# The first feed-forward product of a hybrid decoder block, 24 of its 32 column tiles by Strassen's seven products

## The chip, the cores and the metric

The kernel runs on one core of a Trainium2 chip. The metric is the time of one execution in microseconds of the device. A core has a matrix engine (TensorE), VectorE, ScalarE, GpSimd and SyncE (SP), whose queue issues all data transfers here. The engines run at the same time, each in the order in which its instructions were issued, and wait for one another by semaphores. TensorE adds its products up in eight banks (PSUM) of 128 partitions by 512 numbers; everything else lies in the on-chip memory (SBUF).

## What is computed

One decoder layer on 512 tokens of width 1024: token mixing (a gated unit and sparse attention), cross-attention into 256 memory tokens, and a feed-forward part. The change concerns the last:

```python
D_MODEL, SEQ, D_FF = 1024, 512, 4096
h = rms_norm(x, norm_ffn_g[l])                                    # (512, 1024)
x = x + jnp.square(jax.nn.relu(h @ w_ff1[l])) @ w_ff2[l]          # w_ff1 1024 x 4096, w_ff2 4096 x 1024
```

All inputs and the output are float32.

## The kernel before

**Numbers.** TensorE's operands are tiles of the type fp32r. Each operand is split into a high part, the number cast to that type, and a low part, the rest (a subtraction on VectorE). A product of two split operands is three matmuls: high by high, high by low, low by high (`mm3`). `split_any` lets the cast go to ScalarE or VectorE; the low part is always VectorE's.

**Order.** The program is written down as a list of operations. The class `Plan` gives each a cost (`cost`), a start from the engines' and buffers' state, and places those with a choice (`nc.either`) on the engine that is done first. `LEADS` moves the priority of single stages; its keys are the names of stages. `issue` then sends out the instructions in the order that came out, so that nearly all carry the same line number in the profile (L412), and groups are told apart by the tiles' names.

**Buffers.** `raw` (3) holds a weight block of 128x1024 as loaded, `w` (4, `WRING`) its two parts. `b8` (11 of 8 KB a partition) holds large tiles: the transposed hidden input, the residual, the hidden activations. `q` (4), `z` (6), `P` (6) and `bT` (2) hold tiles 512 wide. `SHARE` says how many of each kind a part of the program (its queue) may hold for sure.

**Feed-forward.** `ch_f(t)` norms token tile t (128 tokens), transposes it and splits it into `h3h` and `h3l`, each two tiles of four 128-row blocks by 512 tokens. For each of the 32 column tiles f of `w_ff1` (128 columns), `granule` loads 1024x128 weights and splits them, `ff1` multiplies, 8 k-blocks by 3 terms with 512 tokens as moving columns: 24 matmuls into one bank. ScalarE takes the relu out of the bank into a `z` tile, and the square goes to ScalarE or VectorE and into `hid[f]`. The first two column tiles (`ff_a`, `ff_b`) are computed in two halves of 256 tokens, as fillers of the cross-attention's waits. The first-product matmuls carry the names `ps<-b,w` (512 columns) and, for the fillers, `ps<-b,b` (256 columns; attention has that name too).

The second product keeps eight banks `accs` (four token tiles by two halves of the width). For each f it loads `w_ff2`'s rows (`load_ff2`), splits them and `hid[f]` (a `qpair`), and adds 8 x 3 matmuls (`part`, `ps<-w,q`). The last two f are taken bank by bank, and each finished bank is scaled, added to the residual in `xs[t]` and stored:

```python
dve.scalar_tensor_tensor(xv[:, c:c + n], accs[2 * t + blk][:, c:c + n], rf[t], xv[:, c:c + n], OP.mult, OP.add)
dma(out[0, t * P:t * P + P, blk * 512 + c:blk * 512 + c + n], xv[:, c:c + n])
```

Of the kernel before, what the change touches and what calls it, by code (L numbers as in the profile page):

```python
# [9 lines left out]
F32 = mybir.dt.float32  # L10
# [7 lines left out]
P = 128  # L18
# [19 lines left out]
WRING = 4  # L38
QLEAD = 200
# [17 lines left out]
LEADS = {"ch_f0": -304, "ch_norm3": -5448, "ch_o0": 500, "ch_o0.w512.2": 3108, "ch_o1": -1711,  # L57
# [17 lines left out]


class Plan:
# [60 lines left out]
    def cost(self, eng, op, aps, func):  # L138
        n = max(self.width(a) for a, _ in aps)
        if eng == "tensor":  # L140
            if op == "transpose" and all(a.dtype == F32 for a, _ in aps):
                return 109
            return max(25, n / 2.4 + (15 if n > 200 else 7))
# [272 lines left out]
def hybrid_block(ctx, tc, x, mem, norm_mix_g, w_in, sg_ln_g, sg_ln_b, sg_w, sg_b, q_norm_g,  # L416
# [10 lines left out]
    spool = ctx.enter_context(tc.tile_pool(name="small", bufs=1))  # L427
    pps = ctx.enter_context(tc.tile_pool(name="ps", bufs=8, space=PS))
# [15 lines left out]
    def qpair():  # L444
        t = zpool.tile([P, 2, 512], F32R, tag="q", bufs=4, name=nm("q"))
        return t[:, 0, :], t[:, 1, :]

    def b8(shape, dt):
        n = 1
        for s in shape[1:]:  # L450
            n *= s
        assert n <= SB8
        t = bpool.tile([P, n], dt, tag="b8", bufs=11, name=nm("b8"))
        if len(shape) == 3:
            return t.rearrange("p (a b) -> p a b", a=shape[1])
        if len(shape) == 4:
            return t.rearrange("p (a b c) -> p a b c", a=shape[1], b=shape[2])
        return t
# [213 lines left out]
    KL = cpool.tile([P, NKV, 2, T], F32R, name="KL")  # L672
# [145 lines left out]
    Vc = cpool.tile([P, NKV, G, P], F32R, name="Vc")  # L818
# [404 lines left out]
    rf = [None] * TT  # L1223
    def ch_norm(t):
        h2 = b8([P, 2, KT, P], F32R)
        st[t]['h2'] = h2
        norm_T(xs[t], g_mem, [h2[:, 0, 0:4, :], h2[:, 0, 4:8, :]], [h2[:, 1, 0:4, :], h2[:, 1, 4:8, :]])
        e = small(1)
        dve.tensor_scalar(e, stats(xs[t], D), EPS / D, EPS * EPS, OP.mult, OP.add)
        st[t]['e'] = e  # L1230
# [106 lines left out]

    hid = []

    def hid_tile(f):  # L1340
        if f < FT - 4:
            if f % 4 == 0:
                t = b8([P, 4, T], F32)
                hid.extend(t[:, i, :] for i in range(4))
        else:
            hid.append(zpool.tile([P, 512], F32, tag="P", bufs=6, name=nm("hid")))
        return hid[f]
# [29 lines left out]
    for f in range(NFILL, FT):  # L1377
        nc.stage = f"ff{f}"
        hid_tile(f)
        ff1(f, granule(w1v[:, :, f * P:f * P + P]), 0, T)  # L1380

# [4 lines left out]
    def load_ff2(f):  # L1386
        (w,) = granule(w2v[:, f:f + 1, :])
        hh, hl = qpair()
        split_any(hid[f], hh, hl)
        ff2[f] = hh, hl, w  # L1390

    def part(f, t, blk):
# [3 lines left out]
            start=f == 0, stop=f == FT - 1)  # L1396

    for f in range(FT - LAST):
        load_ff2(f)
        for t in range(TT):  # L1400
            for blk in range(2):
                part(f, t, blk)
    for f in range(FT - LAST, FT):
        load_ff2(f)
    for t in range(TT):
        for blk in range(2):
            for f in range(FT - LAST, FT):
                part(f, t, blk)
            xv = xs[t][:, blk * 512:blk * 512 + 512]
# [37 lines left out]
```

## Time and profile before

| | |
|---|---|
| median of 3 runs | 697.59 us (696.68 to 697.99) |
| the profiled execution | 696.73 us, its span from the first to the last instruction 695.0 us |
| TensorE busy, matmuls | 688.1 us (99%), 3600 |
| VectorE, ScalarE, GpSimd busy | 420.8 us (61%), 307.7 us (44%), 80.5 us (12%) |
| loaded and stored | 68.32 MB and 2.10 MB, 101 GB/s over the span |

In the profile PE is a matmul, PEld the load of its weights (the stationary operand), DVE is VectorE, ACT ScalarE, POOL GpSimd, SPq the queue of transfers. A name such as `ps<-b,w` is output, moving operand, stationary operand for a matmul. Matmuls are pipelined: the duration of one is longer than the step to the next, so steps are read from starts.

### The profile page before, as it was taken

The page shows a single profiled execution, that of the slowest core. Times are in us where ns is not written, and L with a number is a line of the kernel's source. Part 1 is how long each engine was busy: PE and PEld are TensorE (multiplying, and loading weights), DVE is VectorE, ACT ScalarE, POOL GpSimd, SP SyncE. Part 2 cuts the span into 40 slices and gives each one's busy share as a digit, 9 for nine tenths or more (in the row PEclk, how much of TensorE's full clock was granted, in tenths as well). Part 3 has the DMA queues.
Part 4 walks back from the last instruction along what each step waited for, and adds up shares of the span by engine and source line. Part 5 has one row for each costly group of instructions (what it writes and reads, how often), then busy time and mean ns, then how long its engine had stood idle before and what let it go on. Part 6 is the DMA issues. An engine that isn't in the chain of part 4 may idle for free.

```text
span 695.0 us, 9606 instructions
## 1 busy us (share of the span) xinstructions
PE 688.1 (99%) x3600; PEld 583.3 (84%) x3600; DVE 420.8 (61%) x832; ACT 307.7 (44%) x622; POOL 80.5 (12%) x121
## 2 busy tenths in 40 slices
PE   8999999999999999999999999999999999999997
PEld 7898887888899888889888888888888888888886
DVE  5698799988999997588832533332233444334433
ACT  6453575977789774677431522221151221112210
POOL 1102123133332230213100000000000000000000
PEclk9999999999999999999999999999999999999999
DMA  8632574560221101323243333333233222333203
GB/s 269 181 112 77 158 203 135 202 188 2 91 92 61 62 1 34 119 62 91 68 112 97 88 95 106 103 91 91 92 108 104 91 91 91 101 109 94 91 1 121
DMA packets 63678, 71.03 MB, mean 102 GB/s; under 512 B 3160, under 2 KB 46928, under 8 KB 63632
## 3 DMA queue, kind: packets, MB, share of 16 engines
q1 hardware_dynamic: 63632, 70.42, 32.8%
q8 instruction: 28, 0.46, 0.3%
q14 instruction: 18, 0.15, 0.1%
HBM read 68.32 MB, written 2.10 MB: 101 GB/s over the span
## 4 chain that ended last, share of the span: by engine, by line
PE 98%; DVE 1%; DMA 1%; ACT 0%; issue 0%; SPq 0%; DVEq 0%
PE ps L412 98%; DMA raw<-in_w_in_dram 1%; DVE b L412 0%; DVE w L412 0%; ACT w L412 0%; SPq L412 0%; ACT z L412 0%; DVEq L1442 0%
## 5 line engine op out<-in xcount | busy, mean ns | idle before, releaser
L412 PE MATMUL ps<-w,q 128*128 128x512 f32 x960 | 224.7, 391 | 0.0
L412 PEld LDWEIGHTS ps<-w,q 128*128 128x128 f32 x960 | 178.9, 188 | 36.4 <-ACT q L412 0.2
L412 PE MATMUL ps<-w,b 128*128 128x512 f32 (+2 forms) x832 | 184.6, 375 | 0.1
L412 DVE TENSOR_TENSOR w<-raw,w 128x1024 fp32r<-128x1024 f32 (+2 forms) x113 | 132.8, 1178 | 69.4 <-ACT w L412 68.4
L412 ACT CAST w<-raw 128x1024 fp32r<-128x1024 f32 (+2 forms) x80 | 82.2, 1029 | 206.7 <-PE ps L412 201.9
L412 PE MATMUL ps<-b,w 128*128 128x512 f32 x720 | 167.1, 390 | 0.0
L412 PEld LDWEIGHTS ps<-w,b 128*128 128x128 f32 (+1 forms) x832 | 143.7, 186 | 25.7 <-DVE w L412 0.6
L412 PEld LDWEIGHTS ps<-b,w 128*128 128x128 f32 x720 | 134.7, 188 | 28.4 <-ACT z L412 0.5
L412 DVE TENSOR_TENSOR b<-ps,b 128x512 fp32r<-128x512 f32 (+2 forms) x88 | 54.7, 636 | 11.2 <-ACT b L412 8.2
L412 PE MATMUL ps<-b,b 128*128 128x256 f32 (+1 forms) x344 | 59.1, 291 | 0.0
L412 DVE CAST q<-b 128x512 fp32r<-128x512 f32 (+1 forms) x28 | 11.7, 418 | 75.8 <-PE ps L412 75.8
L412 ACT CAST b<-ps 128x512 fp32r<-128x512 f32 (+1 forms) x84 | 43.9, 548 | 20.5 <-PE ps L412 20.3
L412 DVE CAST w<-raw 128x1024 fp32r<-128x1024 f32 (+2 forms) x33 | 21.5, 652 | 51.4 <-PE ps L412 51.1
L412 ACT ACTIVATE z<-ps 128x512 f32<-128x512 f32 (+3 forms) x43 | 23.6, 580 | 62.8 <-PE ps L412 62.8
L412 PEld LDWEIGHTS ps<-b,b 128*128 128x128 f32 x344 | 48.0, 190 | 1.5 <-DVE b L412 0.2
L412 POOL TENSOR_SCALAR P<-P,s,gates 128x128 f32<-128x128 f32 (+3 forms) x56 | 35.6, 645 | 96.0 <-DVE s L412 62.0
L412 POOL TENSOR_TENSOR r<-s,negh 128x1 f32<-128x1 f32 (+2 forms) x25 | 23.4, 939 | 106.2 <-DVE s L412 106.2
L412 PE MATMUL ps<-idf,P 128*128 128x128 f32 x192 | 30.9, 276 | 0.0
L412 PE MATMUL ps<-b,q 128*128 128x256 f32 (+2 forms) x96 | 25.8, 334 | 0.3 <-ACT q L412 0.3
L412 PEld LDWEIGHTS ps<-idf,P 128*128 128x128 f32 x192 | 22.5, 141 | 2.4 <-POOL P L412 0.3
L412 DVE TENSOR_TENSOR q<-b,q 128x512 fp32r<-128x512 f32 (+1 forms) x36 | 23.5, 656 | 1.4 <-ACT q L412 0.5
L412 ACT ACTIVATE P<-P,s 128x384 f32<-128x384 f32 (+1 forms) x32 | 21.6, 676 | 1.8 <-DVE s L412 1.5
(156 smaller groups left out, 561.2 us busy)
## 6 DMA issues: line engine op xcount, KB each, us to landing
raw<-in_w_ff_dram SPq DMA_DIRECT2D x64, 512.0 KB, 3.7
raw<-in_w_in_dram SPq DMA_DIRECT2D x12, 512.0 KB, 4.5
raw<-in_cmp_w_dram SPq DMA_DIRECT2D x8, 512.0 KB, 4.3
raw<-in_w_out_dram SPq DMA_DIRECT2D x8, 512.0 KB, 4.1
raw<-in_w_mkv_dram SPq DMA_DIRECT2D x8, 512.0 KB, 4.4
b<-in_x_dram SPq DMA_DIRECT2D x8, 256.0 KB, 5.2
raw<-in_w_in_dram SPq DMA_DIRECT2D x8, 256.0 KB, 5.5
b<-in_x_dram SPq DMA_DIRECT2D x4, 512.0 KB, 7.0
```

The source lines that it names most:

```text
L412: getattr(getattr(self.nc, eng), op)(*a, **k)
```

## The change

Column tiles 8 to 31 are taken four at a time. The hidden input is cut into two halves of the tokens (256) and two of k (512), the weights of four column tiles into two halves of k and two of the columns (256), and the 2x2 product of blocks is made of seven products in place of eight (Winograd's order, with sums S1 to S4 of the input, made once, and three running sums of the weights in each group). A product (`prod`) is 2 column tiles by 4 k-blocks by 3 terms, 24 matmuls of 256 columns into one bank. Four banks serve a group; three of the seven products are added onto a bank that has been read before. The sums of products are made by VectorE out of the banks, relu and square follow (`relu2`).

Each weight block (512x256, 512 KB) is loaded and, as it is or as a sum, split: seven splits in a group in place of four. The residual `xs[t]` is written to DRAM (`xq`) behind `ch_f(t)` and read back into new tiles (`xr`) for the end. The hidden tiles lie in `bT`, `P`, `b8`, `q` and a gain row's buffer; the second product takes f in the order 20 to 27, 0 to 19, 28 to 31, and its first eight splits of `hid` use `b8` tiles. `b8` has 12 buffers in place of 11 and `q` 5 in place of 4; `KL` and `Vc` of the attention, which had tiles of their own, use these. `LEADS` is new throughout, and the plan's cost of a matmul of 201 to 300 columns is 4 ns less.

```diff
--- before.py
+++ after.py
@@ -36,6 +36,8 @@
 LAST = 2
 NWARM = 28
 WRING = 4
+
+FONE = 8
 QLEAD = 200
 SB8 = 2048
 
@@ -54,24 +56,30 @@
          "wa": dict(w=3, raw=2),
          "wf": dict(w=1, raw=1)}
 
-LEADS = {"ch_f0": -304, "ch_norm3": -5448, "ch_o0": 500, "ch_o0.w512.2": 3108, "ch_o1": -1711,
...
+LEADS = {"ch_f0": -3007, "ch_norm0": -637, "ch_norm1": -2138, "ch_norm2": 916, "ch_norm3": 2082,
...
 
 
 class Plan:
@@ -140,7 +148,7 @@
         if eng == "tensor":
             if op == "transpose" and all(a.dtype == F32 for a, _ in aps):
                 return 109
-            return max(25, n / 2.4 + (15 if n > 200 else 7))
+            return max(25, n / 2.4 + (15 if n > 300 else 11 if n > 200 else 7))
         if eng == "sync":
             run = min(list(a.ap)[-1][1] for a, _ in aps)
             return max(450, 4 * n * max(list(a.ap)[0][1] for a, _ in aps) / (230 if run <= 128 else 290))
@@ -425,6 +433,7 @@
     bpool = ctx.enter_context(tc.tile_pool(name="big", bufs=1))
     zpool = ctx.enter_context(tc.tile_pool(name="z", bufs=1))
     spool = ctx.enter_context(tc.tile_pool(name="small", bufs=1))
+    dpool = ctx.enter_context(tc.tile_pool(name="dram", bufs=1, space=bass.MemoryType.DRAM))
     pps = ctx.enter_context(tc.tile_pool(name="ps", bufs=8, space=PS))
 
     dma = nc.sync.dma_start
@@ -442,7 +451,7 @@
         return zpool.tile([P, 512], dt, tag="z", bufs=6, name=nm("z"))
 
     def qpair():
-        t = zpool.tile([P, 2, 512], F32R, tag="q", bufs=4, name=nm("q"))
+        t = zpool.tile([P, 2, 512], F32R, tag="q", bufs=5, name=nm("q"))
         return t[:, 0, :], t[:, 1, :]
 
     def b8(shape, dt):
@@ -450,7 +459,7 @@
         for s in shape[1:]:
             n *= s
         assert n <= SB8
-        t = bpool.tile([P, n], dt, tag="b8", bufs=11, name=nm("b8"))
+        t = bpool.tile([P, n], dt, tag="b8", bufs=12, name=nm("b8"))
         if len(shape) == 3:
             return t.rearrange("p (a b) -> p a b", a=shape[1])
         if len(shape) == 4:
@@ -669,7 +678,7 @@
 
 
     KB = b8([P, NKV, 2, T], F32R)
-    KL = cpool.tile([P, NKV, 2, T], F32R, name="KL")
+    KL = b8([P, NKV, 2, T], F32R)
     for h in range(NKV):
         pool.memset(KL[(1 - h) * HD:(2 - h) * HD, h].bitcast(F32), 0.0)
     VB = b8([P, 2 * NKV * TT, P], F32R)
@@ -815,7 +824,9 @@
 
     nc.lead, nc.stage = 0, "cmp"
 
-    Vc = cpool.tile([P, NKV, G, P], F32R, name="Vc")
+    Vc = zpool.tile([P, 1024], F32R, tag="q", bufs=5, name="Vc")
+    nc.home[Vc.tensor.name] = "gain"
+    Vc = Vc.rearrange("p (h g d) -> p h g d", h=NKV, g=G)
     pool.memset(Vc.bitcast(F32), 0.0)
 
     cps = bank().rearrange("p (i c) -> p i c", i=2)
@@ -1221,6 +1232,7 @@
     g_ffn = h3h = h3l = wq = wmo = None
     st = [dict() for _ in range(TT)]
     rf = [None] * TT
+    xq = [dpool.tile([P, D], F32, name=f"xq{t}") for t in range(TT)]
     def ch_norm(t):
         h2 = b8([P, 2, KT, P], F32R)
         st[t]['h2'] = h2
@@ -1335,15 +1347,29 @@
         rf[t] = cpool.tile([P, 1], F32, name=f"rf{t}")
         dve.tensor_tensor(rf[t], r, r, OP.mult)
 
+        dma(xq[t], xs[t])
+
     hid = []
 
+    def hid_tiles(f):
+
+        if f < 2:
+            return [zpool.tile([P, 512], F32, tag="bT", bufs=2, name=nm("hid")) for _ in range(2)]
+        if f < 8:
+            return [zpool.tile([P, 512], F32, tag="P", bufs=6, name=nm("hid")) for _ in range(6)]
+        if f < 20:
+            t = b8([P, 4, T], F32)
+            return [t[:, i, :] for i in range(4)]
+        t = [zpool.tile([P, 2, 512], F32, tag="q", bufs=5, name=nm("hid")) for _ in range(1 if f == 28 else 2)]
+        if f == 28:
+            g = cpool.tile([P, 2, 512], F32, tag="gain", bufs=1, name=nm("hid"))
+            nc.home[g.tensor.name] = "gain"
+            t.append(g)
+        return [v[:, i, :] for v in t for i in range(2)]
+
     def hid_tile(f):
-        if f < FT - 4:
-            if f % 4 == 0:
-                t = b8([P, 4, T], F32)
-                hid.extend(t[:, i, :] for i in range(4))
-        else:
-            hid.append(zpool.tile([P, 512], F32, tag="P", bufs=6, name=nm("hid")))
+        while len(hid) <= f:
+            hid.extend(hid_tiles(len(hid)))
         return hid[f]
 
     def ff1(f, ws, c0, n):
@@ -1374,18 +1400,135 @@
     nc.queue, nc.stage = "ff", "ff"
 
 
-    for f in range(NFILL, FT):
+    for f in range(NFILL, FONE):
         nc.stage = f"ff{f}"
         hid_tile(f)
         ff1(f, granule(w1v[:, :, f * P:f * P + P]), 0, T)
 
+
+    def quarter(th, kh):
+        c = slice(th * 2 * P, th * 2 * P + 2 * P)
+        return h3h[kh][:, :, c], h3l[kh][:, :, c]
+
+    def half(t, i):
+        return t[:, i, :].rearrange("p (k n) -> p k n", k=4)
+
+    def either_tt(out, a, b, op):
+        nc.either(("vector", "tensor_tensor"), ("gpsimd", "tensor_tensor"))(out, a, b, op)
+
+    nc.stage = "ffs"
+    X, Y, Z = (b8([P, 2, 1024], F32) for _ in range(3))
+    A22, A21, A11, A12 = quarter(1, 1), quarter(1, 0), quarter(0, 0), quarter(0, 1)
+    for t, i, (h, l) in ((X, 0, A21), (X, 1, A22), (Y, 0, A11), (Y, 1, A12)):
+        either_tt(half(t, i), h.bitcast(F32), l.bitcast(F32), OP.add)
+    sums = []
+
+    def keep(t, i):
+        w = b8([P, 2, 1024], F32R)
+        split_any(t[:, i, :], w[:, 0, :], w[:, 1, :])
+        sums.append((half(w, 0), half(w, 1)))
+
+    either_tt(Z[:, 0, :], X[:, 0, :], X[:, 1, :], OP.add)
+    keep(Z, 0)
+    either_tt(Z[:, 1, :], Z[:, 0, :], Y[:, 0, :], OP.subtract)
+    keep(Z, 1)
+    either_tt(X[:, 0, :], Y[:, 0, :], X[:, 0, :], OP.subtract)
+    keep(X, 0)
+    either_tt(Y[:, 1, :], Y[:, 1, :], Z[:, 1, :], OP.subtract)
+    keep(Y, 1)
+    S1, S2, S3, S4 = sums
+
+    def raw4():
+        t = wpool.tile([P, 1024], F32, tag="raw", bufs=3, name=nm("raw"))
+        nc.home[t.tensor.name] = wqueue[0]
+        return t
+
+    def pair(t):
+        w = wpool.tile([P, 2, 1024], F32R, tag="w", bufs=WRING, name=nm("w"))
+        nc.home[w.tensor.name] = wqueue[0]
+        split_any(t, w[:, 0, :], w[:, 1, :])
+        return half(w, 0), half(w, 1)
+
+    def prod(ps, A, W, first):
+
+        (ah, al), (wh, wl) = A, W
+        for i in range(2):
+            c = slice(i * P, i * P + P)
+            o = ps[:, i * 2 * P:i * 2 * P + 2 * P]
+            for k in range(4):
+                on = dict(start=False, stop=False, skip_group_check=not first)
+                nc.tensor.matmul(o, wh[:, k, c], ah[:, k, :], **dict(on, start=first and i == 0 and k == 0))
+                nc.tensor.matmul(o, wh[:, k, c], al[:, k, :], **on)
+                nc.tensor.matmul(o, wl[:, k, c], ah[:, k, :], **dict(on, stop=i == 1 and k == 3))
+
+    def relu2(src, f, th):
+
+        r = ztile()
+        act(r, src, AF.Relu)
+        for i in range(2):
+            nc.either(("scalar", "square"), ("vector", "square"))(
+                hid[f + i][:, th * 2 * P:th * 2 * P + 2 * P], r[:, i * 2 * P:i * 2 * P + 2 * P])
+
+    ts = b8([P, 2, 1024], F32)
+    for f in range(FONE, FT, 4):
+        nc.stage = f"ff{f}"
+        hid_tile(f)
+
+        def load_w(kh, fh):
+            t = raw4()
+            c = (f + 2 * fh) * P
+            dma(t.rearrange("p (k n) -> p k n", k=4), w1v[:, 4 * kh:4 * kh + 4, c:c + 2 * P])
+            return t
+
+        b11, b12 = load_w(0, 0), load_w(0, 1)
+        p1, p5, p6, p7 = bank(), bank(), bank(), bank()
+        w = pair(b11)
+        t = ts[:, f // 4 % 2, :]
+        nc.stage = f"ff{f}.1"
+        either_tt(t, b12, b11, OP.subtract)
+        prod(p1, A11, w, True)
+        c1 = ztile()
+        nc.scalar.copy(c1, p1)
+        prod(p5, S1, pair(t), True)
+        nc.stage = f"ff{f}.2"
+        b22 = load_w(1, 1)
+        either_tt(b12, b22, b12, OP.subtract)
+        either_tt(t, b22, t, OP.subtract)
+        prod(p6, S2, pair(t), True)
+        u2 = ztile()
+        dve.tensor_tensor(u2, p6, c1, OP.add)
+        nc.stage = f"ff{f}.3"
+        prod(p7, S3, pair(b12), True)
+        v = ztile()
+        dve.tensor_tensor(v, p5, u2, OP.add)
+        nc.stage = f"ff{f}.4"
+        b21 = load_w(1, 0)
+        either_tt(t, b21, t, OP.subtract)
+        prod(p1, A12, pair(b21), False)
+        relu2(p1, f, 0)
+        dve.tensor_tensor(v, p7, v, OP.add)
+        relu2(v, f + 2, 1)
+        nc.stage = f"ff{f}.5"
+        prod(p5, S4, pair(b22), False)
+        v = ztile()
+        dve.tensor_tensor(v, p5, u2, OP.add)
+        relu2(v, f + 2, 0)
+        nc.stage = f"ff{f}.6"
+        prod(p7, A22, pair(t), False)
+        dve.tensor_tensor(u2, p7, u2, OP.add)
+        relu2(u2, f, 1)
+
     nc.stage = "ff2"
     accs = [bank() for _ in range(2 * TT)]
     ff2 = {}
 
     def load_ff2(f):
         (w,) = granule(w2v[:, f:f + 1, :])
-        hh, hl = qpair()
+        if order.index(f) < 8:
+            t = b8([P, 2, 512], F32R)
+            hh, hl = t[:, 0, :], t[:, 1, :]
+        else:
+            hh, hl = qpair()
         split_any(hid[f], hh, hl)
         ff2[f] = hh, hl, w
 
@@ -1393,20 +1536,27 @@
         hh, hl, (wh, wl) = ff2[f]
         c = slice(blk * 512, blk * 512 + 512)
         mm3(accs[2 * t + blk], [(hh[:, t * P:t * P + P], hl[:, t * P:t * P + P])], [(wh[:, c], wl[:, c])],
-            start=f == 0, stop=f == FT - 1)
-
-    for f in range(FT - LAST):
+            start=f == order[0], stop=f == order[-1])
+
+
+    order = [*range(20, 28), *range(20), *range(28, 32)]
+    for f in order[:-LAST]:
         load_ff2(f)
         for t in range(TT):
             for blk in range(2):
                 part(f, t, blk)
-    for f in range(FT - LAST, FT):
+    for f in order[-LAST:]:
         load_ff2(f)
+    nc.stage = "xr"
+    xr = [b8([P, 2, D], F32) for _ in range(2)]
+    for t in range(TT):
+        dma(xr[t // 2][:, t % 2, :], xq[t])
+    nc.stage = "ff2"
     for t in range(TT):
         for blk in range(2):
-            for f in range(FT - LAST, FT):
+            for f in order[-LAST:]:
                 part(f, t, blk)
-            xv = xs[t][:, blk * 512:blk * 512 + 512]
+            xv = xr[t // 2][:, t % 2, blk * 512:blk * 512 + 512]
             n = 256 if t == TT - 1 and blk else 512
             for c in range(0, 512, n):
                 dve.scalar_tensor_tensor(xv[:, c:c + n], accs[2 * t + blk][:, c:c + n], rf[t], xv[:, c:c + n],
```

## Rows read from the trace of the kernel before

**Rows 1.** The profile page, parts 1 and 2: busy us of each engine; 40 slices of the span.

```profile
PE 688.1 (99%) x3600; PEld 583.3 (84%) x3600; DVE 420.8 (61%) x832; ACT 307.7 (44%) x622; POOL 80.5 (12%) x121
...
DVE  5698799988999997588832533332233444334433
...
PEclk9999999999999999999999999999999999999999
```

**Rows 2.** The chain that ended last, in order of time: start us, us, what.

```profile
7.61 121.52 PE ps L412 x666
...
131.98 377.87 PE ps L412 x2083
```

**Rows 3.** Windows by stage: length; PE, PEld, DVE, ACT, POOL busy; clock, DMA share, GB/s.

```profile
0.00:8.00 8.00, 5.95 (x41) 4.88 (x42) 3.78 (x10) 3.34 (x5) 3.42 (x9) 1.00 0.71 207
...
120.00:132.00 12.00, 10.91 (x68) 9.35 (x66) 10.46 (x24) 10.44 (x17) 0.99 (x2) 1.00 0.28 89
132.00:200.00 68.00, 68.00 (x415) 58.51 (x416) 61.91 (x168) 50.71 (x146) 21.34 (x37) 1.00 0.40 130
...
349.00:392.00 43.00, 43.00 (x208) 36.13 (x207) 12.34 (x16) 10.68 (x15) 0.55 (x1) 1.00 0.35 99
392.00:517.00 125.00, 124.95 (x551) 103.18 (x550) 43.84 (x48) 37.21 (x61) 0.00 (x0) 1.00 0.32 96
517.00:692.00 175.00, 174.27 (x769) 143.96 (x767) 71.66 (x95) 31.32 (x31) 0.00 (x0) 1.00 0.27 89
```

**Rows 4.** Timeline of TensorE, 395 us to the end: start us, us, what, xcount.

```profile
394.75 122.45 PE L412 MATMUL ps<-b,w 128*128 128x512 f32 x538
517.03 174.24 PE L412 MATMUL ps<-w,q 128*128 128x512 f32 x768
```

**Rows 5.** Timeline of TensorE, same columns: two runs of 256 columns, and what follows each.

```profile
344.21 3.69 PE L412 MATMUL ps<-b,b 128*128 128x256 f32 x29
347.74 0.86 PE L412 MATMUL ps<-w,q 128*128 128x512 f32 x3
...
359.32 1.48 PE L412 MATMUL ps<-b,b 128*128 128x256 f32 x11
360.63 0.63 PE L412 MATMUL ps<-b,w 128*128 128x512 f32 x2
```

**Rows 6.** Timeline of TensorE where 256 and 512 columns alternate.

```profile
383.78 0.28 PE L412 MATMUL ps<-b,b 128*128 128x256 f32 x1
383.89 0.40 PE L412 MATMUL ps<-b,w 128*128 128x512 f32 x1
...
384.84 0.28 PE L412 MATMUL ps<-b,b 128*128 128x256 f32 x1
```

**Rows 7.** Groups by form: us busy, mean ns of one, idle time before and its releasers.

```profile
L412 DVE TENSOR_TENSOR w<-raw,w 128x1024 fp32r<-128x1024 f32 x102 | 124.6, 1223 | 64.6 <-ACT w L412 63.7
L412 ACT CAST w<-raw 128x1024 fp32r<-128x1024 f32 x74 | 78.0, 1054 | 204.9 <-PE ps L412 201.9 <-DMA raw<-in_cmp_w_dram 1.8 <-DMA raw<-in_w_in_dram 1.0
...
L412 DVE TENSOR_TENSOR b<-ps,b 128x512 fp32r<-128x512 f32 x64 | 42.7, 685 | 8.5 <-ACT b L412 8.2
...
L412 DVE CAST w<-raw 128x1024 fp32r<-128x1024 f32 x28 | 19.4, 692 | 49.4 <-PE ps L412 49.2
L412 ACT ACTIVATE z<-ps 128x512 f32<-128x512 f32 x34 | 19.3, 606 | 53.0 <-PE ps L412 53.0
...
L412 POOL TENSOR_TENSOR z<-b 128x512 f32<-128x512 f32 x4 | 5.5, 1366 | 7.0 <-ACT b L412 5.8 <-DVE cmk L412 1.2
...
L412 ACT COPY z<-ps 128x256 f32<-128x256 f32 x8 | 3.0, 378 | 2.2 <-PE ps L412 2.1
```

**Rows 8.** The profile page, part 6: a weight load's KB and us from issue to landing.

```profile
raw<-in_w_ff_dram SPq DMA_DIRECT2D x64, 512.0 KB, 3.7
```

**Rows 9.** Timeline of TensorE: the last transposes of the feed-forward's input.

```profile
354.65 0.60 PE L412 MATMUL ps<-idf,z 128*128 128x128 f32 x4
```

**Rows 10.** Timeline of TensorE's weight loads at the seam of the two products.

```profile
511.46 5.31 PEld L412 LDWEIGHTS ps<-b,w 128*128 128x128 f32 x24 [0.47 <-ACT z L412]
```

40 rows, old and new, of the table LEADS are left out of this document.

## The prediction

> **What bounds the kernel now.** I read the page first: TensorE is busy 688.1 of 695.0 us and its clock is granted in full throughout (2.4 GHz), while VectorE's busy digits fall from 5 to 9 in the first half to 2 to 5 in the second [rows 1, 3]. Then the chain of work that ended last: it is TensorE from 7.6 us to 691.3 us but for two short places, 129.13 to 131.98 and 509.85 to 511.46 us [rows 2, 4, 10]. So time is gained where TensorE has less to stream, and lost where it is made to wait. Third the windows by stage: in the feed-forward stages (349 to 692 us) TensorE is busy 43.00 of 43, 124.95 of 125 and 174.27 of 175 us, VectorE and ScalarE at most 41% of each, GpSimd not at all from 392 us on [rows 3]. The reader is to see two things there: the work that the change adds outside TensorE falls where there is room, and from 132 to 200 us, with VectorE at 61.91 and ScalarE at 50.71 of 68 us, TensorE still lost nothing. Last the single matmuls. A full column tile is 24 matmuls of 512 columns; 538 of them take 122.45 us and 768 of the second product 174.24 us [rows 4], that is (122.45 - 0.39) / 537 = 0.227 us from start to start, the last one's 0.39 us being its drain. For 256 columns, two unbroken runs give 1.31 us over 11 steps and 3.53 over 29 (start of the run to start of what follows) [rows 5]: 0.119 and 0.122 us. Half the columns cost 53% of the time, not half.
>
> **Product by product.** Removed: tiles 8 to 31 as full tiles, 24 x 24 = 576 matmuls x 0.227 = 130.8 us. Added: six groups of four tiles, each seven products of 2 column tiles x 4 k-blocks x 3 terms = 168 matmuls of 256 columns, in all 1008. I take 0.120 us, between the two runs: 121.0 us. TensorE is 9.8 us lighter. The bounds: the runs themselves give 119.9 and 123.0 us (10.8 and 7.8 us saved). Where 256 and 512 columns alternate one by one, three pairs take 384.84 - 383.78 = 1.06 us [rows 6]; less 3 x 0.227 that is 0.126 us a half, 127.0 us in all and 3.8 us saved. The step from such a half to the full matmul behind it is as short as 0.11 us [rows 6]: 110.9 us and 19.9 us saved. The groups are unbroken runs, as in [rows 5], so 0.120 is the nearest.
>
> The Trainium skill ("TensorE: Matmul & The Clock Gate", Back-to-back issue gap) gives a warm matmul its columns at 2.4 GHz plus 2.5 ns, 109 ns for 256 and 216 ns for 512. By it the edit would save 576 x 0.2158 - 1008 x 0.1092 = 14.2 us; the rows disagree with it by 11 ns at both widths, and the smaller matmuls pay that twice as often.
>
> **Work for the other engines, for one group (20.2 us of TensorE).** VectorE must do seven low parts of 128x1024 at 1.22 us and five additions out of a bank (512 wide, like the low parts of 0.69 us in [rows 7]): 8.6 + 3.4 = 12.0 us. The four weight sums (128x1024, two inputs, 1.22) add 4.9 us if none goes to GpSimd: 16.9 us, 84%. ScalarE has one copy and four relus at 0.61 and, if it takes all of them, seven high parts at 1.05 and eight squares of 256 columns at 0.38: 3.0 + 7.4 + 3.0 = 13.4 us, 66% [rows 7]. That is below what stood beside an unbroken TensorE from 132 to 200 us (91% and 75%) [rows 3], so I cost it at nothing. What hides it is the ring of four split weights: one product's weights last 24 x 0.120 = 2.88 us, and the chain sum, high part, low part (1.22 + 1.05 + 1.22 = 3.5 us) may run up to three products ahead. Without that cover each of the 42 products would wait 0.6 us, 26 us together.
>
> The raw ring has three slots and the group's third block stays in its slot until the sixth product. Counting from a group's start, the next group's first block finds its slot once the fourth product's weights are split (from 0 us on, by 8.6 at the latest) and is first needed at 11.5 us; with 3.7 us to land [rows 8] and some 2.3 us for the split it is there. The second finds its slot at about 5 us and is needed at 14.4, the third at 8 and 17.3: at least 5 us to spare each. Cost nothing; if one were late, the first product of a group would be. Bytes are the same: 24 loads of 512 KB instead of 24.
>
> The sums of the hidden input, once: eight additions and four low parts of 128x1024, 12 x 1.22 = 14.7 us of VectorE, and 4.2 us of casts. The input is whole once the last transposes before 355.3 us are split [rows 9], six full tiles (32.7 us of TensorE) come ahead of the first group, and from 349 to 392 us VectorE is busy 12.34 of 43 us [rows 3]. Covered, with some 16 us to spare; uncovered, the second product would be late by those 14.7 us.
>
> **Residual through DRAM.** Four writes and four reads of 512 KB stand on SP's queue beside the weights. A write waits for its token tile's last addition, and behind it on SP wait the loads of the next column tiles; the raw ring and the split ring cover several tiles of 5.4 us each, and a load lands in 3.7 us. The DMA engines are busy 0.32 of the time in these stages [rows 3] and 4 MB more is a few per cent of it. The reads must be there for the last additions, 170 us after they can be issued. Nothing either way; the end (last matmul to last store) keeps its form.
>
> **The seam and the rest.** The first eight splits of the second product take their buffers from the input and its sums, the first of which come free after the last group's first two products, some 14 us ahead of need: nothing. Tile 20, first in the new order, was finished a group earlier, so the old seam's wait at 511 us, at most 0.47 us [rows 10], need not recur. All start orders before the feed-forward are new as well, with KL and Vc in shared buffers. Of the 6.9 us in which TensorE is idle [rows 1], 2.05 lie before 8 us, 1.09 from 120 to 132 us, 0.78 from 392 to 692 us [rows 3] and 3.0 behind: about 1 us to win. What a worse order costs no row shows; the nearest are the two broken places of the chain, 2.85 and 1.61 us [rows 2, 10], so up to 4.5 us to lose. I take 0.6 us lost for both, nearer to nothing because TensorE held at VectorE loads above those of now.
>
> **Sum.** 696.73 us (the profiled execution: a span of 695.0 and 1.7 around it) - 9.8 + 0.6 = 687.5. The median of the runs is 0.86 above the profiled one: **688.4 us**.
>
> **Rivals.**
> 1. *Steps nearer to half.* If the 256-column matmuls ran at the 0.11 us of [rows 6], 19.9 us would go: 677.7 us in the median. The runs of 11 and 29 speak against it. I put 677.5 to 684 here, most of it near the top, where the steps shorten by a few ns only. The rule of the Trainium skill quoted above would give 696.73 - 14.2 + 0.86 = 683.4 us.
> 2. *Half of the gain is given back.* Steps of 0.126 us, or the 4.5 us of broken places: 696.73 - 3.8 + 0.9 = 693.8, or 688.4 + 3.9 = 692.3 us. For it: the whole order is new and each product now hangs on sums. 690.5 to 696.2.
> 3. *Weight preparation becomes the pace* (the other side). If the three products of look-ahead are lost, each product takes the chain's 3.5 us instead of 2.88: 42 x 3.5 = 147 us against 130.8, so 697.59 + 16 = 714 us. It decides from 9.8 / 42 = 0.23 us of wait a product on. It could come about on VectorE: with all casts there too (0.69 each) it has 16.9 + 4.8 = 21.7 us a group, as long as four tiles take now, and with squares more. GpSimd is no sure way out: one 512-wide addition takes it 1.37 us [rows 7]. Against it: ScalarE has room for the casts, and each is placed on whichever engine is done first.
> The Trainium skill ("Perfetto Trace Analysis", Optimizing Scalar/DVE Operations) warns that GpSimd and VectorE share a read port, so that handing sums over may not help; no row of before has the two at it in this stage.
> 4. *No effect*: gain and waits cancel, 696.2 to 699.0 us.
>
> **How the numbers follow.** About 0.2% (1.4 us) is what a measurement of this kernel can tell from no change. The forecast, 684 to 690.5 us, 687.8 with no wait at all: 0.60. Rival 1: 0.10. Rival 2: 0.19. Rival 4: 0.04. Rival 3: 0.07. Hence faster 0.89, same 0.04, slower 0.07. The range of 682.5 to 694 us holds the forecast, three quarters of rival 2 (0.14) and the top of rival 1 (0.05), 0.79 in all; the forecast's own range is the 684 to 690.5 us above.
>
> **What would show it.** Right: runs of 256-column matmuls at 0.119 to 0.122 us a step, a group in 20 to 20.5 us, TensorE unbroken from the first group to the end, VectorE at 75 to 90% and ScalarE at 50 to 70% there, and the stages ahead as long as now within 1.5 us. Wrong: idle time of TensorE's weight loads that ends with a low part, a sum or a raw load; steps of 0.125 us or more; a first group that starts later than six tiles after the input; stages before 349 us that grew by over 2 us.

## The result, and the profile after

The changed kernel takes **690.69 us** in the median of five runs (688.54 to 692.88), the kernel before 697.59: a ratio of 0.9897, 95% interval 0.9869 to 0.9926. That is faster by 1.0% and 2.3 us above the forecast value of 688.4: inside the prediction's range of 682.5 to 694 us, but 0.2 us above the 684 to 690.5 us that it called the forecast's own. The profiled execution took 688.54 us, its span 686.5 us; before, 696.73 and 695.0.

The profile page of the changed kernel, parts 1 and 2, against [rows 1]:

```profile
PE 678.4 (99%) x4032; PEld 595.8 (87%) x4032; DVE 495.3 (72%) x912; ACT 340.9 (50%) x681; POOL 75.1 (11%) x120
...
DVE  6596898988899998579699587898957233344423
...
PEclk9999999999999999999999999999999999999999
```

There are 432 matmuls more (1008 for 576) and 9.7 us less of TensorE's busy time. VectorE's hump now reaches past the middle, where the groups are.

The timeline of TensorE from the first group to the second product (start us, us, what, count) answers to [rows 4] and [rows 5]:

```profile
376.45 127.68 PE L420 MATMUL ps<-b,w 128*128 128x512 f32 x1019
503.96 6.99 PE L420 MATMUL ps<-w,b 128*128 128x512 f32 x30
510.79 4.59 PE L420 MATMUL ps<-b,w 128*128 128x256 f32 x37
515.22 37.02 PE L420 MATMUL ps<-w,b 128*128 128x512 f32 x162
```

The last 37 matmuls of 256 columns take 515.22 - 510.79 = 4.43 us, 0.120 each. The other 971 share the first row with 48 full ones: 971 x 0.120 + 48 x 0.227 = 127.4 us, and the row lasts 503.96 - 376.45 = 127.51. So TensorE hardly waited in any group of this profile. The second product starts inside the last group; its first eight steps now move `w` against `b8` tiles and are named `ps<-w,b`.

Its windows by stage and then by group (length; PE, PEld, DVE, ACT, POOL busy; clock, DMA share, GB/s), against [rows 3]:

```profile
0.00:8.00 8.00, 5.59 (x41) 4.64 (x42) 3.84 (x10) 3.35 (x5) 3.42 (x9) 1.00 0.72 200
8.00:74.00 66.00, 65.66 (x359) 56.54 (x358) 48.93 (x95) 33.52 (x63) 6.48 (x13) 1.00 0.51 153
74.00:92.00 18.00, 17.51 (x107) 15.29 (x106) 15.62 (x32) 7.88 (x11) 1.50 (x1) 1.00 0.61 186
...
115.00:134.00 19.00, 17.91 (x104) 14.95 (x103) 17.46 (x39) 17.28 (x29) 0.73 (x2) 1.00 0.48 151
...
347.00:376.50 29.50, 29.50 (x159) 25.45 (x158) 27.20 (x32) 11.31 (x16) 2.00 (x2) 1.00 0.45 136
...
427.76:447.92 20.16, 20.16 (x170) 20.16 (x169) 17.25 (x19) 7.70 (x11) 0.00 (x0) 1.00 0.35 106
447.92:468.08 20.16, 20.16 (x170) 20.16 (x169) 18.01 (x22) 12.21 (x22) 0.00 (x0) 1.00 0.34 104
```

The reader is to see three things. A group lasts 20.16 us with VectorE at 86 to 89% and ScalarE at 38 to 61% of it. With the sums of the input VectorE is busy 27.20 of 29.5 us between 347 and 376.5 us, and TensorE loses nothing there. What TensorE loses it loses early: 2.41 us before 8 us, 0.34 and 0.49 us up to 92 us, 1.09 us around 125 us.

The groups by form between 430 and 500 us show where VectorE's time goes; none of the sums went to GpSimd, and some casts went to VectorE:

```profile
L420 DVE TENSOR_TENSOR w<-raw,w 128x1024 fp32r<-128x1024 f32 x15 | 18.1, 1218 | 0.8 <-ACT w L420 0.8
L420 DVE TENSOR_TENSOR w<-b,w 128x1024 fp32r<-128x1024 f32 x9 | 11.0, 1224 | 2.1 <-ACT w L420 2.0
L420 DVE TENSOR_TENSOR b<-raw,b 128x1024 f32<-128x1024 f32 x7 | 8.6, 1223 | 0.2
L420 DVE CAST w<-b 128x1024 fp32r<-128x1024 f32 x5 | 3.5, 695 | 1.4 <-PE ps L420 1.1
```

The chain that ended last answers to [rows 2]. From 209.87 us it is one piece of TensorE to the end; ahead of that it has more breaks than before, one with a transfer in it. (A break of the chain is not idle time: the chain is off TensorE from 77.1 to 90.1 us, and TensorE idles 0.49 us there.)

```profile
82.48 5.14 DMA raw<-in_cmp_w_dram
...
90.09 27.65 PE ps L420 x148
...
209.87 472.94 PE ps L420 x2839
```

### The profile page after: what moved, and what is told of

Its sections match the earlier page's. It is cut to its first block, busy times and chain, and to the rows that moved or that the text cites. A ratio compares the mean times of both kernels' runs of the same rounds, so it can differ in the third digit from the quotient of the medians.

```text
span 686.5 us, 10617 instructions
## 1 busy us (share of the span) xinstructions
PE 678.4 (99%) x4032; PEld 595.8 (87%) x4032; DVE 495.3 (72%) x912; ACT 340.9 (50%) x681; POOL 75.1 (11%) x120
## 4 chain that ended last, share of the span: by engine, by line
PE 94%; DVE 2%; ACT 2%; DMA 1%; issue 0%; SPq 0%; DVEq 0%; ACTq 0%
PE ps L420 94%; DVE w L420 1%; DMA raw<-in_cmp_w_dram 1%; ACT b L420 1%; ACT L420 1%; DVE b L420 1%; DMA raw<-in_w_in_dram 1%; ACT w L420 0%; DVE s L420 0%; SPq L420 0%; DVEq L1592 0%; ACT pc L420 0%; DVE pt L420 0%; ACT KC L420 0%; ACTq L420 0%
## 5 line engine op out<-in xcount | busy, mean ns | idle before, releaser
L420 PE MATMUL ps<-w,b 128*128 128x512 f32 (+3 forms) x1024 | 230.6, 378 | 0.9 <-DVE w L420 0.5
L420 PEld LDWEIGHTS ps<-w,b 128*128 128x128 f32 (+1 forms) x1024 | 178.6, 186 | 33.6 <-DVE w L420 1.3
L420 ACT CAST w<-raw 128x1024 fp32r<-128x1024 f32 (+1 forms) x92 | 94.4, 1027 | 189.4 <-PE ps L420 175.7
L420 PE MATMUL ps<-w,q 128*128 128x512 f32 x768 | 180.3, 391 | 0.0
L420 PEld LDWEIGHTS ps<-w,q 128*128 128x128 f32 x768 | 143.0, 188 | 28.8
L420 PE MATMUL ps<-b,w 128*128 128x256 f32 (+1 forms) x1152 | 155.0, 296 | 0.0
L420 ACT CAST b<-ps 128x512 fp32r<-128x512 f32 (+2 forms) x88 | 45.9, 549 | 20.7 <-PE ps L420 20.2
L420 POOL TENSOR_SCALAR P<-P,s,gates 128x256 f32<-128x256 f32 (+3 forms) x55 | 34.9, 643 | 96.1 <-DVE s L420 90.1
L420 DVE TENSOR_TENSOR z<-ps,z 128x512 f32<-128x512 f32 (+2 forms) x39 | 24.6, 631 | 2.7 <-PE ps L420 1.4
L420 PEld LDWEIGHTS ps<-b,q 128*128 128x128 f32 x144 | 22.9, 190 | 2.3 <-DVE pt L420 0.2
```

Of the source, the lines that this page charges most:

```text
L420: getattr(getattr(self.nc, eng), op)(*a, **k)
```

## The experiments

In each the changed kernel is the base, unless it says otherwise. Times are medians; ratios are against runs of the kernel before on the same chip.

**The same kernel again**, no edit.

> The changed kernel once more, for a second profile and five more pairs of times. Theory A (the seven products save TensorE's time and hide everything else): five inner groups at 20.16 us each again, 688.5 to 691 us; where this profile differs from the first one by more than 0.5 us, the difference lies ahead of 347 us, in the places where TensorE stood idle in the first (74 to 92 and 115 to 134 us). Rival C (VectorE, busy 18.1 of 20.16 us a group, is at its edge and falls behind in some executions): products longer than 2.88 us inside the groups, at different places from profile to profile, 1 to 3 us in all.

Measured: 690.38 us (689.54 to 691.86), ratio 0.9883 (0.9866 to 0.9900). Groups as before, but for the second:

```profile
82.88 5.54 DMA raw<-in_cmp_w_dram
...
90.88 37.22 PE ps L420 x194
```

```profile
423.16 22.02 PEld L420 LDWEIGHTS ps<-b,w 128*128 128x128 f32 x183 [0.23 <-DVE w L420]
```

(the chain, then the timeline of the weight loads). The profiles differ by 1.0 us of span: 0.4 us is a transfer that landed in 5.54 in place of 5.14 us, 0.2 us one wait in a group; the other 0.4 us lies ahead of 14 us, where the chain starts with another load and TensorE's first piece ends at 13.70 in place of 13.30 us. Theory A holds. C is right in that one place, to 0.2 us; the run without writes, below, shows the same place with a longer wait.

**Half columns without the seven products** (the kernel before; only `ff1` changes):

```diff
-        mm3(ps, ws, kpairs(h3h, h3l, c0, n))
+        for c in range(0, n, 2 * P if f >= 8 else n):
+            m = 2 * P if f >= 8 else n
+            mm3(ps[:, c:c + m], ws, kpairs(h3h, h3l, c0 + c, m))
```

> The kernel before, with column tiles 8 to 31 in two halves of 256 tokens, both in one bank, nothing else changed: eight products of half width, the price of narrow matmuls without the seven products. Theory A: 24 x (48 x 0.120 - 24 x 0.227) = 7.5 us more than before, 705 us. If a half cost half (rival: the step follows the columns alone): 697.6 us. If the alternating bound of 0.126 us held in unbroken runs: 14.4 us more, 712 us.

Measured: 706.04 us, ratio 1.0104 (1.0086 to 1.0122), 7.3 us above the 698.73 us of the kernel before in these runs. One row of TensorE's timeline gives the step, (80.44 - 0.28) / 668 = 0.120 us, the last matmul's 0.28 us being its drain:

```profile
399.81 80.44 PE L412 MATMUL ps<-b,w 128*128 128x256 f32 x669
```

From this step 7.5 us were worked out. This is what the narrower matmuls cost; the eighth product left out must first pay for it.

**All casts and squares of the groups on VectorE:**

```diff
-        split_any(t, w[:, 0, :], w[:, 1, :])
+        dve.tensor_copy(w[:, 0, :], t)
+        dve.tensor_tensor(w[:, 1, :], t, w[:, 0, :].bitcast(F32), OP.subtract)
...
-            nc.either(("scalar", "square"), ("vector", "square"))(
+            dve.square(
```

> The changed kernel with all 42 high parts and all squares of the groups on VectorE, that is rival 3 of the prediction made true. VectorE then has, by the durations, 8.6 + 3.4 + 4.9 + 4.8 + 3.4 = 25.1 us of work a group, or, with the step from one to the next some 8% below the durations, 22.5 to 23.5 us. If VectorE then sets the pace: groups of 22.5 to 25 us, 12 to 29 us more than the changed kernel, 703 to 720 us, so no faster than before. If TensorE keeps the pace: 690 us, groups of 20.2 us.

Measured: 715.92 us, ratio 1.0240 (1.0222 to 1.0259). Windows of its third to fifth group, columns as above:

```profile
438.37:459.57 21.20, 20.40 (x170) 20.20 (x169) 20.99 (x28) 1.74 (x3) 0.00 (x0) 1.00 0.31 94
459.57:481.67 22.10, 21.08 (x171) 20.32 (x169) 22.07 (x35) 4.72 (x8) 0.00 (x0) 1.00 0.26 78
481.67:510.66 28.99, 23.51 (x168) 22.14 (x169) 25.26 (x31) 1.22 (x2) 0.00 (x0) 0.94 0.30 92
```

In the third and fourth group VectorE is full, and TensorE waits. In the fifth VectorE itself waits for a weight block, and behind the waits of TensorE the clock falls, to 0.94 over the group:

```profile
493.76 1.23 DVE L420 TENSOR_TENSOR b<-raw,b 128x1024 f32<-128x1024 f32 x1 [2.82 <-DMA raw<-in_w_ff_dram]
```

Rival 3 is a real mechanism; by the durations it had 25 us of VectorE's work a group here where there are 18. That the time comes out near the prediction's 714 us is luck: that sum let each product wait 0.6 us for want of cover, and here the groups last from 21.2 to 29.0 us for several causes.

**Only the casts on VectorE** (the first half of that edit):

> The changed kernel with the 42 high parts of the groups on VectorE, the squares free to choose. VectorE has 12.0 + 4.9 + 7 x 0.69 = 21.7 us a group by the durations, 19.8 us by the step from one to the next (1.14, 0.60, 0.61 us). If the step counts, TensorE keeps the pace in most groups: 691 to 694 us. If the durations count: 1.6 us more a group than 20.16, some 9 us, 700 us, the point from which rival 3 of the prediction decides.

Measured: 695.50 us, ratio 0.9965 (0.9955 to 0.9976), 5 us above the changed kernel and between the two expectations. The weight loads' timeline has two waits in the second group, and the windows show the clock behind them:

```profile
415.19 5.57 PEld L420 LDWEIGHTS ps<-b,w 128*128 128x128 f32 x46 [1.41 <-DVE w L420]
422.88 0.66 PEld L420 LDWEIGHTS ps<-b,w 128*128 128x128 f32 x5 [2.12 <-ACT z L420]
```

```profile
424.00:428.00 4.00, 4.00 (x23) 4.00 (x22) 3.64 (x5) 0.00 (x0) 0.00 (x0) 0.57 0.33 98
```

So VectorE's step from one instruction to the next counts, not the sum of the durations: at 21.7 us by the durations, VectorE is busy 19.96 of 20.23 and 19.76 of 20.25 us in the third and fourth group, and these and the last keep the pace of the changed kernel; the fifth is 1.2 us longer. But the second is 5.2 us longer, by two late products and the clock, while VectorE is busy 17.50 of the 20 us from 404 to 424: the margin is that of the first single piece that is late.

**The four weight sums on GpSimd** (`pool.tensor_tensor` in place of `either_tt` inside the groups):

> The changed kernel with the four weight sums of each group on GpSimd. VectorE falls from 18.1 to some 13.2 us a group; GpSimd has four additions of 128x1024 at about 2.6 us, an estimate from twice the 1.37 us of one of 512 columns. Theory A (VectorE is in the shadow already): 690 to 691.5 us, no gain from the relief, because no group waits for it now. Rival (the Trainium skill's shared read port: while GpSimd adds, VectorE's two-input subtractions wait): VectorE's subtractions grow by up to 10 us a group in total, products longer than 2.88 us, 695 us or more.

Measured: 697.89 us, ratio 1.0006 (0.9986 to 1.0026): the whole gain is gone. Groups by form, 430 to 500 us:

```profile
L420 PEld LDWEIGHTS ps<-b,w 128*128 128x128 f32 x554 | 66.8, 192 | 3.4 <-DVE w L420 1.4 <-ACT w L420 1.3 <-ACT z L420 0.7
L420 POOL TENSOR_TENSOR b<-raw,b 128x1024 f32<-128x1024 f32 x8 | 21.8, 2731 | 19.6 <-DVE w L420 13.9 <-issue 5.7
L420 DVE TENSOR_TENSOR w<-raw,w 128x1024 fp32r<-128x1024 f32 x13 | 21.5, 1679 | 3.7 <-ACT w L420 3.7
```

The low parts of loaded blocks take 1679 ns each in place of 1218, and a sum 2731 ns in place of 1223. VectorE was relieved of 4.9 us a group and TensorE was made to wait, 3.4 us in these 70 us where it waited 0.0 before: the warning of the Trainium skill ("Perfetto Trace Analysis", Optimizing Scalar/DVE Operations) agrees with these rows. What share of the loss comes from the longer subtractions, and what from the sums themselves being ready later, no run separates.

**No products** (`FONE = 32`, sums and groups left out):

> The changed kernel without the products and their sums: all 30 column tiles as full tiles, everything else as changed (buffers, start priorities, residual through DRAM, order of the second product). Theory A (the groups' shorter stream is all of the gain): 690.5 + 9.8 = 700.3 us, so slower than the kernel before by 1 to 3 us, the price of the rest of the change. Rival B (the new order of the stages or the seam brings part of the gain): 692 to 697 us.

Measured: 703.59 us, ratio 1.0082 (1.0066 to 1.0099), 3.3 us beyond theory A. The weight loads' timeline has two waits that neither kernel has:

```profile
423.10 3.99 PEld L420 LDWEIGHTS ps<-b,w 128*128 128x128 f32 x18 [2.05 <-ACT z L420]
...
522.99 2.17 PEld L420 LDWEIGHTS ps<-w,b 128*128 128x128 f32 x10 [2.05 <-ACT z L420]
```

A step is 2.02 us at each in place of 0.227, 3.6 us in all. Without them, by this reckoning, it would be 700.0 us, 9.5 us above the changed kernel: theory A's 9.8. Why the relu is late there was not traced; this order was not found for full tiles, and a fresh search of the priorities for the kernel before was not run. The rest of the change (priorities, buffers, residual) so costs some 2 us against the kernel before, 697.92 us in these runs. Rival B falls.

**The old start priorities** for all stages ahead of the full column tiles (`LEADS` of before there, of after from `ff2` on):

> The changed kernel with the old start priorities for all stages ahead of the full column tiles, the new ones for the column tiles and groups only. Theory A (the gain is the groups'; the new order ahead of them gives about 1 us back): the gain stays, 688 to 692 us, groups of 20.16 us. Rival B (a good part of the gain comes from the re-ordered stages): 693 to 697 us.

Measured: 701.97 us, ratio 1.0048 (1.0030 to 1.0067). Neither expectation: 11.5 us are lost. The windows ahead of the groups:

```profile
0.00:130.00 130.00, 127.64 (x691) 108.64 (x692) 99.91 (x205) 71.82 (x130) 21.38 (x32) 1.00 0.52 159
130.00:140.00 10.00, 7.79 (x60) 6.52 (x59) 8.81 (x21) 7.23 (x19) 1.75 (x4) 1.00 0.56 206
140.00:250.00 110.00, 109.87 (x674) 94.60 (x673) 100.82 (x281) 82.55 (x224) 31.45 (x50) 1.00 0.25 83
250.00:280.00 30.00, 27.37 (x184) 23.80 (x183) 25.55 (x68) 20.13 (x51) 5.16 (x8) 0.98 0.00 1
...
330.00:365.00 35.00, 32.79 (x206) 28.00 (x205) 27.06 (x51) 19.44 (x41) 5.57 (x11) 1.00 0.35 111
```

TensorE idles 2.2 us, 2.6 us and 2.2 us from 130 to 140, 250 to 280 and 330 to 365 us, where the old priorities meet the new buffers. Behind them the third to fifth group last 20.16 us as ever; the second has one wait of 1.02 us for a low part. In all TensorE idles 14.9 us (702.6 - 687.7), 6.8 more than in the changed kernel; the clock is 0.98 from 250 to 330 us, and the rest of the loss was not traced. So re-found priorities are no gain by themselves (the run without products), but old ones would have cost more than the products bring.

**No writes of the residual** (the four `dma(xq[t], xs[t])` left out, the reads taken from `xd`):

> The changed kernel without the four writes of the residual; the reads stay, but fetch the block's input x in place of it, so the output lacks what the first two sub-layers add. Theory A (the way through DRAM is hidden): the same time as the changed kernel, 690 to 691.5 us, groups at 20.16 us. Rival (the writes wait on SP's queue for the last additions and hold up the weights behind them): 1 to 3 us less.

Measured: 690.57 us, ratio 0.9892 (0.9872 to 0.9911): nothing, as theory A has it. (The reads stayed; none of them is in the changed kernel's chain, but no run is without them.) This profile caught the wait in the second group at its longest. The timelines of SP, VectorE and the weight loads there:

```profile
413.89 0.37 SPq L420 DMA_DIRECT2D raw<-in_w_ff_dram  x1
```

```profile
420.48 1.23 DVE L420 TENSOR_TENSOR b<-raw,raw 128x1024 f32<-128x1024 f32 x1 [1.46 <-DMA raw<-in_w_ff_dram]
421.63 1.22 DVE L420 TENSOR_TENSOR w<-b,w 128x1024 fp32r<-128x1024 f32 x1
422.76 0.68 DVE L420 TENSOR_TENSOR z<-ps,z 128x512 f32<-128x512 f32 x1
423.36 1.22 DVE L420 TENSOR_TENSOR w<-raw,w 128x1024 fp32r<-128x1024 f32 x1
```

```profile
424.63 20.45 PEld L420 LDWEIGHTS ps<-b,w 128*128 128x128 f32 x170 [1.57 <-DVE w L420]
```

A weight block issued at 413.89 us landed 6.5 us later, at 420.4, in place of the median's 3.8; the sum waited 1.46 us for it. Behind the sum on VectorE stands the low part of another block, done at 424.58 us, and TensorE had waited 1.57 us for that one.

**Seven groups** (`FONE = 4`):

> The changed kernel with tiles 4 to 31 in seven groups in place of six. One more group saves 1.6 us by theory A: 688.9 us, if the input's sums (14.7 us of VectorE) are ready in time, with two full tiles and one product of cover in place of six tiles. If they are late, the second product waits up to 8 us for them and the time is 690 to 697 us.

Measured: 692.92 us, ratio 0.9927 (0.9912 to 0.9942). The sums are late, as the second expectation has it, and a second place follows (the weight loads' timeline):

```profile
373.38 48.98 PEld L420 LDWEIGHTS ps<-b,w 128*128 128x128 f32 x406 [2.03 <-DVE w L420]
423.70 0.30 PEld L420 LDWEIGHTS ps<-b,w 128*128 128x128 f32 x2 [1.34 <-ACT w L420]
424.70 15.42 PEld L420 LDWEIGHTS ps<-b,w 128*128 128x128 f32 x128 [0.71 <-ACT z L420]
```

The first wait ends with the low part of a weight sum. On VectorE's timeline it stands behind the sums of the input:

```profile
361.89 6.89 DVE L420 TENSOR_TENSOR b<-b,b 128x1024 f32<-128x1024 f32 x6
...
372.11 1.22 DVE L420 TENSOR_TENSOR w<-b,w 128x1024 fp32r<-128x1024 f32 x1
```

**Priorities searched anew**, with six groups and with seven; in both the plan's price of a matmul is set to the measured steps:

```diff
-            return max(25, n / 2.4 + (15 if n > 300 else 11 if n > 200 else 7))
+            return max(25, n / 2.4 + (13.7 if n > 200 else 7))
```

> The changed kernel with the start priorities searched anew, six groups as before, and the plan's price of wide matmuls set to the measured steps (0.120 and 0.227 us). Theory A leaves nothing to win inside the groups; what the order can still give are the waits of 0.6 to 1.5 us ahead of 347 us and at the first group, 3 to 4 us together: 687 to 690 us. If these waits come from late transfers and not from the order: 690.5 us.

> Seven groups (tiles 4 to 31) with the start priorities searched anew and the same prices. If the late sums of the seven-group run were a matter of order, its 4.9 us of waits at 370 and 422 us go, and the seventh group's 1.6 us come through: 692.9 - 4.9 = 688.0 us, and 685 to 688 us with the waits ahead of the groups shortened too, the fastest of all. If the 14.7 us of sums can't be hidden behind two full tiles in any order: 690 us or more.

Measured: 693.07 us, ratio 0.9929 (0.9917 to 0.9942), and 689.59 us, ratio 0.9883 (0.9868 to 0.9897). With six groups the search missed: the kernel is 2.5 us slower than the changed one. With seven groups the late sums are gone, so they were a matter of order: the weight loads' timeline, up to 410 us, is one row from 373.51 us on (the next wait is one of 0.28 us at 442.88).

```profile
373.51 36.58 PEld L447 LDWEIGHTS ps<-b,w 128*128 128x128 f32 x303
```

But both lose ahead of the groups. The window from 115 to 142 us, of the changed kernel and then of the two:

```profile
115.00:142.00 27.00, 25.91 (x152) 21.94 (x151) 25.02 (x64) 24.93 (x57) 5.53 (x11) 1.00 0.52 178
```

```profile
115.00:142.00 27.00, 24.36 (x143) 20.20 (x142) 24.62 (x58) 24.25 (x55) 3.22 (x7) 1.00 0.45 155
```

```profile
115.00:142.00 27.00, 24.07 (x142) 19.83 (x140) 25.54 (x62) 23.34 (x56) 4.43 (x9) 1.00 0.50 168
```

TensorE idles 1.6 and 1.8 us longer there. Seven groups have the lowest median of all, but their interval lies inside that of the changed kernel's own runs; whether they are faster is open.

## Why the prediction was right, step by step

- **The step of 0.120 us** held exactly, and with it the 9.8 us. The run with half columns and no products (+7.3 us) and the run without products (700.0 us net of its two waits) show it from both sides. Rival 1's step and the 109 ns that the prediction quotes from the Trainium skill ("TensorE: Matmul & The Clock Gate", Back-to-back issue gap) stand in no unbroken run of 256-column matmuls here.
- **The other engines' work in the shadow** was right, and its size nearly: 16.9 us of VectorE a group were worked out and 17.3 and 18.0 measured in the two groups shown, since the plan put some casts there too; ScalarE so had 38% in one of them, less than the 50 to 70% named as a sign. That it costs nothing is shown by the unbroken groups; where it would begin to cost is shown by the two runs with casts on VectorE: 5 us for 3.7 us more a group, 25 us for 7.
- **The raw ring's "at least 5 us to spare"** failed in one place. In the second group a block's load was issued 5.4 us after the group's start, about when the step had it, but landed 6.5 us later, and TensorE waited 1.57 us in that profile and 0.2 us at the same place in another. The step assumed the median landing, and it weighed each block by itself: the sum that waited for this block held up another block's low part behind it on VectorE. Why this landing took so long is open; another load had been issued 2 us ahead of it, but other loads of the groups, 1 to 2 us behind one, landed in 4.5 to 5.0 us.
- **The sums of the input** were hidden behind the six tiles, and cost some us with two tiles until the order was found again. **The residual's writes to DRAM** are free: without them the time is the same.
- **The new order elsewhere** was given 0.6 us. It cost 1.2: TensorE idles 8.1 us in all (686.5 - 678.4) in place of 6.9. The profiled execution came out at 688.54 where 687.5 was forecast, 1.0 us more: 0.6 of it is this, 0.3 lies outside the span (2.0 us around it, where 1.7 was taken over), and 0.1 is TensorE's busy time, 9.7 us less in place of 9.8. The bound of 4.5 us to lose was too small for a worse order: with the old priorities 11.5 us are lost. No row of before shows such a cost, and the two broken places taken as nearest were no measure of it.
- **From the profiled execution to the median** 0.86 us were added, and it was 2.15: the profiled run was the fastest of five, and the changed kernel's runs spread over 4.3 us, five runs of the kernel before beside them over 2.2 (696.67 to 698.83). Two places that hang on a transfer differ between its profiles: the wait ahead of 90 us and the one in the second group. They account for 0.6 of the 1.0 us between two profiles, the first 14 us for the rest; the spread of the other runs was not traced.

The 2.3 us between forecast and result are these last two terms, 1.0 and 1.3 us: of a forecast gain of 9.2 us, 6.9 came. They carry the median 0.2 us past the forecast's own 690.5 us, into the band that the prediction left to rival 2. The second set of runs has 690.38 us, so on which side of that line the median falls is chance. Of rival 2's causes, the step of 0.126 us is not there, and of the 4.5 us of broken places 1.2 came.

## What to carry to other kernels

A kernel that streams on one engine all the time gains what is taken from that stream, and the step must be read at the new width: seven of eight products are 12.5% less, but at 0.120 us a half in place of 0.114 only 7.5% of the 131 us came through. Before work is put in another engine's shadow, look for the first single piece of it that is late, since that can break the stream while the engine still has room. And when a change alters the buffers under a tuned order, the order has to be found again: its price (11.5 us here) can exceed the gain, and no profile of the old kernel shows it.

## What the runs showed of the hardware

- After two waits of TensorE's weight loads of 1.41 and 2.12 us, the granted clock between 424 and 428 us was 0.57 on average: it had fallen to 1.2 GHz for most of that stretch, and was 1.00 again behind it. In the run with seven groups two waits of 1.34 and 0.71 us, in the group of the same tiles, left it at 1.00. Such a stretch makes a short wait cost more than its length: 23 matmuls of 256 columns ran in these 4 us, where 33 fit at 0.120 us.
- Two-input subtractions of VectorE on SBUF grew from 1218 to 1679 ns on average while GpSimd added on SBUF, and GpSimd's addition of 128x1024 took 2.5 to 3.0 us, so GpSimd was no second VectorE for this work.
- The landing of one weight block of 512 KB ran to 6.5 us, against a median of 3.8; the cause is open.
